# A hybrid decoder step on one core: moving rows at multiples of 64 bytes, norms summed tile by tile between blocks, another order for the WKV phase

## The chip, the cores and the metric

The kernel runs on one core of a Trainium2 chip. The metric is device time in microseconds of one execution; less is better. The kernel before takes 2849.76 us, the median of 3 runs (2849.45 to 2850.34).

## The reference, cut to what matters

One inference step of a decoder trunk with two layers. Layer 0 mixes with RWKV-7, layer 1 with RG-LRU (a gated linear recurrence); each is followed by a causal ConvFFN. Two request groups share the weights: a prompt of 256 tokens and 8 sample rows with carried state, so T = 264 columns. The model is 2048 wide, the FFN 5632.

```
for i in range(2):
    sh_m, sc_m, gt_m, sh_f, sc_f, gt_f = split(silu(c) @ w_mod[i] + b_mod[i])
    h = rms_norm(x, g0) * (1 + sc_m) + sh_m
    out, state = rwkv7_time_mix(h, ...) if i == 0 else rglru_block(h, ...)
    x = x + gt_m * rms_norm(out, g1)
    h = rms_norm(x, g2) * (1 + sc_f) + sh_f
    gt, u = h @ w_gate, h @ w_up
    f = (gelu(causal_dwconv(gt)) * u) @ w_down
    x = x + gt_f * rms_norm(f, g3)
```

The step returns x for both groups and all states (WKV matrices, shift rows, recurrence and convolution states).

## The kernel before, in words

The activations lie with channels on the 128 partitions and the 264 tokens along the row: U0 (the residual) and U1 (a block's output) have 16 tiles of 128 channels. A weight piece is 128 x 1024 numbers, two k-tiles by four output tiles of 128. SyncE loads it raw (L420), ScalarE casts it to a rounded high half wh (L434), and VectorE subtracts to get the low half wl (L435). A ring of four wh and four wl tiles holds split pieces, so a split can run up to four pieces ahead. The moving side is split in the same way (L492, L493) into AH and AL, or ah and al. mm_pieces then issues three products for every pair of k-tile and output tile (L455 wh·xh, L456 wh·xl, L457 wl·xh), 24 matmuls for a piece, into four PSUM banks.

The program is a sequence of stages. Startup loads x (L326), sums its squares over all 16 tiles by matmuls with a matrix of ones (NormPipe, L505 and L506), and computes the first modulation vectors with narrow matmuls against w_mod (wm, L345) and a transpose (L740). Then come the RWKV projections, the WKV phase from about 300 to 713 us, the output projection, and FFN 0 to 1670; the RG-LRU layer to 2021; FFN 1 to 2827; the tail.

The WKV phase is a set of generators, one letter for each kind of job (JOBS), and a text table ORDER says which job takes its next step; with manual_schedule the instructions stand in exactly that order on every engine. Elsewhere the tile framework's scheduler places instructions by their program order and their dependences. Between blocks, w_mod's pieces for later modulation vectors are computed at a fixed pace (wm_pump, paced by mm_group).

Between two blocks lies a junction. out_proj or ffn ends with four groups of pieces; each finished bank is squared (SqAcc.push) and evicted with its gate into U1. The first 12 squares are added up by GpSimd into sqacc, the last four stay apart as tails. rstd_of then sums sqacc and the four tails with five matmuls (L484), takes the square root (L486) and the reciprocal (L488): r1. residual adds U1 * r1 to U0, the sample's columns for all tiles at once (L543, L544), the prompt's two tiles at a time by step on VectorE or GpSimd (L549, L550). residual_and_h then forms the input of the next block without waiting for the next norm: XH and XL hold U0 * sc, split (L580, L581), with the sample's and the shift's columns at the end (xe, L568 to L570), 274 columns; main(p) multiplies piece p with tiles 2p and 2p+1. Beside it the squares of U0 (L577, paired at L582) are summed by norm(p) (L586); after norm(7) the reciprocal r2 (L628) scales the four results, and prep forms AH and AL for all later pieces of the block. There are three such junctions, and the end of the program has the residual part alone.

Of the kernel before, what the change touches and what calls it, by code (L numbers as in the profile page):

```python
# [42 lines left out]
v1 2v0 v1 2s2 2w4 p6 p7 b3 p6 2w5 u4 u5 x1 p6 v1 p6 2v0 2v1 2b2 v0 3q0 d4 b3 v1 q0 2b3 2q0 p7 3b3 q0 2p8 2h0
d4 2p7 p6 2h0 q0 p8 h0 3q0 l8 p8 2p6 b4 4s2 p6 3q0 3b3 p7 s4 p7 2v1 d5 2x2 p7 2l9 3q0 2v2 p7 2v1 p7 q0 h0 v1
2v2 a0 q0 o0 2p6 3p7 w7 2o0 2p6 l11 v3 2p7 2q1 v2 d7 q1 v2 4p9 p8 o0 2h0 2s4 2v2 2q1 v2 2b4 b5 o0 2v2 2p8 v3
a1 3o0 l10 h0 p7 v3 2x2 p9 q0 x2 v3 s4 w6 2s4 4o0 p9 3x2 p8 2x2 w6 p8 2q1 2p8 b4 d6 4q1 b4 2g0 s4 2g0 2p9 3g0
u6 w7 u7 v3 2q1 b4 2g0 3q1 s4 g0 v4 b4 2v4 l10 4v3 d6 d7 2w8 2s6 u8 v4 b4 v3 4q1 2g0 2a0 w9 q0 q1 a0 v3 a0 s6
# [1772 lines left out]
```

## Time and profile before

| what | value |
|---|---|
| median of 3 runs | 2849.76 us (2849.45 to 2850.34) |
| profiled execution | 2848.57 us, span 2846.8 us, mean granted TensorE clock 0.987 |
| TensorE busy | 2740.7 us, 96% of the span |
| VectorE, ScalarE, GpSimd busy | 1753.7, 1358.7, 524.4 us |
| read from memory | 629.42 MB, 226 GB/s over the span |

The span is the time from the first to the last instruction that the profile shows; the execution's time is 1.8 us longer. A busy share is an average over all stages. The chain of waits follows the work that ended last back to what released it, so it tells which engine's time makes up the span.

### The profile page before, as it was taken

The numbers are of one execution on the slowest core, as the hardware profiler recorded it, in microseconds if no ns is written. First come the engines' busy times: TensorE is split into PE (matmuls) and PEld (weight loads), VectorE is DVE, ScalarE is ACT, GpSimd is POOL, SyncE is SP. The second block draws the span as 40 slices with busy tenths as digits, with TensorE's granted clock in tenths as the row PEclk, the third lists the DMA queues.
The fourth block names the chain that finished last, engine by engine and source line by source line (L and its number), as shares of the span: only waits on it lengthen the run. The fifth ranks groups of instructions, "written<-read, shape, count | busy, mean of one in ns | idle before, by whom it ended". The sixth has DMA issues, their size and how long they took to land.

```text
span 2846.8 us, 61582 instructions
## 1 busy us (share of the span) xinstructions
PE 2740.7 (96%) x25820; PEld 2526.2 (89%) x25820; DVE 1753.7 (62%) x2824; ACT 1358.7 (48%) x2187; POOL 524.4 (18%) x1045
## 2 busy tenths in 40 slices
PE   7999999888999999999999999999999999999997
PEld 6899876665989999999999989999899999999997
DVE  5877776876476535545545579775765455455555
ACT  5333435644455434433434459785554444344444
POOL 2111435553121000000000023332210000000002
PEclk9999999999999999999999999999999999999998
DMA  8777558776766666666666665666666555555552
GB/s 330 288 261 244 185 176 246 241 234 215 276 237 232 257 245 238 252 252 255 247 237 252 256 248 199 253 239 237 237 244 252 207 180 178 178 180 184 183 183 76
DMA packets 146566, 648.48 MB, mean 228 GB/s; under 512 B 41152, under 2 KB 60752, under 8 KB 78064
## 3 DMA queue, kind: packets, MB, share of 16 engines
q1 hardware_dynamic: 145216, 641.25, 62.7%
q8 instruction: 202, 3.31, 0.5%
q0 software_dynamic: 1072, 3.30, 0.4%
q14 instruction: 76, 0.62, 0.1%
HBM read 629.42 MB, written 15.07 MB: 226 GB/s over the span
## 4 chain that ended last, share of the span: by engine, by line
PE 86%; DVE 7%; ACT 2%; DMA 2%; issue 1%; POOL 1%; SPq 0%; DVEq 0%; ACTq 0%; POOLq 0%
PE bk L455 18%; PE bk L456 18%; PE bk L457 18%; PE sq L455 7%; PE sq L456 7%; PE sq L457 7%; PE wm L345 5%; DVE wl L435 1%; PE bk L902 1%; ACT wh L434 1%; DVE bt L549 1%; PE bk L908 1%; PE bk L814 0%; PE sq L814 0%; DVE U L550 0%
## 5 line engine op out<-in xcount | busy, mean ns | idle before, releaser
L435 DVE TENSOR_TENSOR wl<-raw,wh 128x1024 fp32r<-128x1024 f32 x444 | 547.6, 1235 | 495.0 <-ACT wh L434 485.8
L434 ACT CAST wh<-raw 128x1024 fp32r<-128x1024 f32 x444 | 464.5, 1048 | 631.6 <-PE bk L456 428.4
L455 PE MATMUL bk<-AH,wh 128*128 128x264 f32 x2352 | 670.6, 285 | 1.4 <-ACT wh L434 1.4
L457 PE MATMUL bk<-AH,wl 128*128 128x264 f32 x2352 | 669.1, 284 | 1.7 <-DVE wl L435 1.6
L456 PE MATMUL bk<-AL,wh 128*128 128x264 f32 x2352 | 668.6, 284 | 0.8 <-DVE AL L493 0.8
L435 DVE TENSOR_TENSOR wl<-rawx,wh 128x1024 fp32r<-128x1024 f32 x310 | 379.3, 1226 | 331.9 <-ACT wh L434 326.8
L434 ACT CAST wh<-rawx 128x1024 fp32r<-128x1024 f32 x310 | 324.4, 1048 | 452.9 <-PE bk L456 332.7
L455 PE MATMUL bk<-ah,wh 128*128 128x264 f32 x1786 | 514.6, 289 | 9.2 <-ACT ah L492 5.5
L457 PE MATMUL bk<-ah,wl 128*128 128x264 f32 x1786 | 510.6, 286 | 0.5 <-DVE wl L435 0.5
L456 PE MATMUL bk<-al,wh 128*128 128x264 f32 x1786 | 510.6, 286 | 0.0
L455 PEld LDWEIGHTS bk<-AH,wh 128*128 128x128 f32 x2352 | 443.3, 188 | 20.7 <-ACT cv L1560 8.4
L457 PEld LDWEIGHTS bk<-AH,wl 128*128 128x128 f32 x2352 | 441.7, 188 | 2.8 <-DVE wl L435 2.8
L456 PEld LDWEIGHTS bk<-AL,wh 128*128 128x128 f32 x2352 | 442.5, 188 | 1.0 <-DVE AL L493 1.0
L455 PEld LDWEIGHTS bk<-ah,wh 128*128 128x128 f32 x1786 | 337.6, 189 | 27.6 <-ACT wh L434 8.1
L457 PEld LDWEIGHTS bk<-ah,wl 128*128 128x128 f32 x1786 | 338.1, 189 | 1.4 <-DVE wl L435 0.8
L456 PEld LDWEIGHTS bk<-al,wh 128*128 128x128 f32 x1786 | 338.4, 189 | 0.6 <-DVE al L493 0.2
L455 PE MATMUL sq<-AH,wh 128*128 128x264 f32 x1040 | 296.7, 285 | 0.1
L456 PE MATMUL sq<-AL,wh 128*128 128x264 f32 x1040 | 295.6, 284 | 0.0
L457 PE MATMUL sq<-AH,wl 128*128 128x264 f32 x1040 | 295.4, 284 | 0.0
L1553 POOL COPY fgs<-gt 128x10 f32<-128x10 f32 x88 | 53.4, 634 | 1307.5 <-ACT gt L1547 1286.2
L455 PEld LDWEIGHTS sq<-AH,wh 128*128 128x128 f32 x1040 | 196.0, 188 | 9.6 <-ACT cv L1560 3.4
L456 PEld LDWEIGHTS sq<-AL,wh 128*128 128x128 f32 x1040 | 195.7, 188 | 0.0
(469 smaller groups left out, 4501.3 us busy)
## 6 DMA issues: line engine op xcount, KB each, us to landing
raw<-in_wst SPq DMA_DIRECT2D x224, 1024.0 KB, 4.9
rawx<-in_wst SPq DMA_DIRECT2D x157, 1024.0 KB, 4.8
raw<-in_wmr SPq DMA_DIRECT2D x72, 1024.0 KB, 7.6
raw<-in_wmr SPq DMA_DIRECT2D x88, 512.0 KB, 5.5
rawx<-in_wmr SPq DMA_DIRECT2D x44, 1024.0 KB, 8.2
raw<-in_wmq SPq DMA_DIRECT2D x23, 1024.0 KB, 4.9
rawx<-in_wmq SPq DMA_DIRECT2D x9, 1024.0 KB, 4.8
lu<-in_lup SPq DMA_DIRECT2D x32, 128.0 KB, 4.8
```

The source lines that it names most:

```text
L345: PE.matmul(ps[32 * g:32 * g + 32, :cols], cs[:, k0 + kk, :], raw[:, (kk * 4 + g) * cols:(kk * 4 + g + 1) * cols], start=(k0 + kk == 0), s ...
L434: S.copy(wh, t)
L435: V.tensor_sub(wl, t, wh.bitcast(F32))
L455: PE.matmul(ps[:, :n], h[:, kk, sl], xh, start=first and kk == 0, stop=False)
L456: PE.matmul(ps[:, :n], h[:, kk, sl], xl, start=False, stop=False)
L457: PE.matmul(ps[:, :n], l[:, kk, sl], xh, start=False, stop=last and kk == 1)
L549: e.tensor_tensor(t, U1[:, j:j + n, :TP], r1[:, None, :TP].to_broadcast([128, n, TP]), op=mult)
L902: PE.matmul(out[HH[(i + turn) % 2]], lhs[HH[i]], rhs[HH[i]], start=start, stop=stop, skip_group_check=True)
L908: PE.matmul(out[q], lhs(r), rhs[r], start=start, stop=stop, skip_group_check=True)
L1553: G.tensor_copy(gs[:, m], gt[:, TP:])
```

## The change

It has five parts.

1. Rows of the moving tiles. AH, AL, ah, al, xh and xl get rows of TA = 272 numbers, of which 264 are used: 1088 bytes instead of 1056. The small tile half grows from 1 to 9 columns, so that what is allocated after it starts at a multiple of 64 bytes. XH and XL (274 columns) stay as they are.
2. ORDER is another permutation of the same jobs for the WKV phase. Which instruction stands where shifts in small steps all through the phase; the set of instructions is the same.
3. Startup: x is loaded in four parts, and all 16 norm steps stand ahead of the modulation pieces.
4. Junctions: in the last group of a block the norm's accumulation begins ahead of the last piece (acc.begin), each bank is squared as soon as its matmuls are issued (hook), the tails are added one by one (add_tail), and the gated evictions of the last two banks wait until after the reciprocal (acc.rest). The two paced pumps stand one piece earlier, and two of the four pumps of the junction move behind its first part. The sample's part is split: VectorE does tiles 0 and 1, GpSimd tiles 2 to 15. The first part of the junction stands in a fixed order on all engines.
5. End: VectorE does all eight residual steps, GpSimd the sample's part, and each step is followed by its output load to memory.

```diff
+TA = 272
...
-s0 g0 p0 l0 2p0 p1 3x0 2l1 l0 p1 g0 5p0 g0 p1 p0 3x0 5p1 p0 w0 p0 l2 2p1 x0 p0 3x0 3p0 2p1 2p0 p2 b0 2p2 2l3
+l0 g0 2p0 s0 x0 g0 2x0 l0 6p0 l1 h0 x0 4p0 2x0 2w0 2p1 b0 l1 3p1 2p0 2p1 l2 3x0 p2 b1 2p1 l2 p1 g0 2p1 p0 2p2
...
-    SP.dma_start(U0[:, :, 1:], I["xT"])
+    for j in range(0, 16, 4):
+        SP.dma_start(U0[:, j:j + 4, 1:], I["xT"][:, j:j + 4])
...
+            if acc and end:
+                acc.begin()
+            mm_pieces(pss, pc, [rhs(2 * q), rhs(2 * q + 1)], q == 0, end, T, hook if end else None)
...
-                elif p == 0:
+                elif p == (2 * pace[0] - 1 if ahead and q >= nk // 2 - 2 else 0):
                     wm_pump(2, False)
-            if ahead and q == nk // 2 - 1:
-                for w in range(ahead):
-                    wm_load(wm_state["i"] + w)
+                    for w in range(ahead):
+                        wm_load(wm_state["i"] + w)
...
+        def begin(s):
+            s.ps = bank()
+            PE.matmul(s.ps[:, :T], onesd, s.acc, start=True, stop=False)
+
+        def add_tail(s, i):
+            PE.matmul(s.ps[:, :T], onesd, s.tail[i], start=False, stop=i == 3)
...
-        step = residual(pool, acc)
-        wm_pump(4)
-        step(V, 0, 2)
-        step(G, 10, 2)
...
-        parts(0)
-        main(0)
-        step(V, 2, 2)
-        step(G, 12, 2)
-        parts(1)
-        norm(0)
-        step(V, 4, 2)
+        with tc.manual_schedule(engines=MANUAL):
+            step, sample = residual(pool, acc)
+            wm_pump(2, False)
+            wm_load(wm_state["i"])
+            wm_load(wm_state["i"] + 1)
+            sample(V, 0, 2)
+            sample(G, 2, 14)
+            step(V, 0, 2)
+            extra(V, 0, 2)
+            halves(0)
+            main(0)
+            step(V, 2, 2)
+            extra(G, 2, 14)
+            halves(1)
+            squares(0)
+            main(1)
+            pairsum(0)
+            step(V, 4, 2)
+            squares(1)
+            pairsum(1)
+            step(G, 10, 2)
+            step(G, 12, 2)
+            norm(0)
+        wm_pump(2, False)
         parts(2)
-        main(1)
...
-            h = a1p([128, T], F32R, "ah", 9)
-            l = a1p([128, T], F32R, "al", 9)
+            h = a1p([128, TA], F32R, "ah", 9)[:, :T]
+            l = a1p([128, TA], F32R, "al", 9)[:, :T]
...
+    for j in range(16):
+        np0.push(U0[:, j, 1:])
     for kp in range(4):
         mod_piece(0, kp)
-        if kp < 2:
-            for j in range(8 * kp, 8 * kp + 8):
-                np0.push(U0[:, j, 1:])
...
+            def hook(m, ps):
+                acc.push(ps[:, :T])
+                if m < 2:
+                    gated(m, ps)
+                else:
+                    acc.rest.append(lambda: gated(m, ps))
+                    acc.add_tail(m - 2)
...
-    AH = ap_([128, 16, T], F32R, "AH")
-    AL = ap_([128, 16, T], F32R, "AL")
+    AH = ap_([128, 16, TA], F32R, "AH")[:, :, :T]
+    AL = ap_([128, 16, TA], F32R, "AL")[:, :, :T]
...
-    for e, j in ((V, 0), (G, 12), (V, 2), (V, 4), (G, 14), (V, 6), (V, 8), (V, 10)):
-        step(e, j, 2)
-    for j in (0, 2, 12, 4, 6, 8, 14, 10):
-        SP.dma_start(O["yT"][:, j:j + 2], U0[:, j:j + 2, 1:])
+    with tc.manual_schedule(engines=MANUAL):
+        step, sample = residual(bp, acc, 8)
+        sample(G, 0, 16)
+        for j in range(0, 16, 2):
+            step(V, j, 2)
+            SP.dma_start(O["yT"][:, j:j + 2], U0[:, j:j + 2, 1:])
```

The line numbers of the kernel after are a little higher: the products are L457 to L459, the casts L436, the low halves L437, the modulation matmuls L347.

How the startup stands on TensorE, from its first matmul, before (L506 is the norm of x, wm the modulation, ah and al the split input):

```order
L506 MATMUL bk<-sq,onesd 128x264 x3
L345 MATMUL wm<-raw,cT 32x128 x16
L506 MATMUL bk<-sq,onesd 128x264 x5
L345 MATMUL wm<-raw,cT 32x128 x16
L506 MATMUL bk<-sq,onesd 128x264 x8
L345 MATMUL wm<-raw,cT 32x128 x16
L345 MATMUL wm<-rawx,cT 32x128 x16
L455 MATMUL bk<-ah,wh 128x264 x4
L455 MATMUL sq<-ah,wh 128x264
```

and after (there the norm is L502):

```order
L502 MATMUL bk<-sq,onesd 128x264 x16
L347 MATMUL wm<-raw,cT 32x128 x48
L347 MATMUL wm<-rawx,cT 32x128 x16
L457 MATMUL bk<-ah,wh 128x264
L458 MATMUL bk<-al,wh 128x264
L457 MATMUL bk<-ah,wh 128x264
L458 MATMUL bk<-al,wh 128x264
L457 MATMUL bk<-ah,wh 128x264
```

All 16 norm matmuls come first, then the 64 modulation matmuls in one run; in the first piece the product with al comes second instead of sixth.

ScalarE at the first junction, from the square root of the norm on, before (XH is the scaled input of the next block, sqb the squares, wh the high half of a weight piece):

```order
L486 ACTIVATE sd<-sq,epsn 128x264
L580 ACTIVATE XH<-U_78,mod_11379 128x256
L569 CAST XH<-xe 128x16x18
L577 ACTIVATE sqb<-U_78 128x528
L580 ACTIVATE XH<-U_78,mod_11379 128x256 x2
L577 ACTIVATE sqb<-U_78 128x528
L580 ACTIVATE XH<-U_78,mod_11379 128x256 x5
L577 ACTIVATE sqb<-U_78 128x528
L580 ACTIVATE XH<-U_78,mod_11379 128x256 x2
L577 ACTIVATE sqb<-U_78 128x528
L580 ACTIVATE XH<-U_78,mod_11379 128x256 x2
L434 CAST wh<-rawx 128x1024 x2
```

and after:

```order
L546 ACTIVATE rs_11701<-sq,epsn 128x264
L1540 ACTIVATE U_10837<-bk,mod_7040 128x256 x2
L590 CAST XH<-xe 128x2x18
L584 ACTIVATE XH<-U_78,mod_11382 128x256 x2
L436 CAST wh<-rawx 128x1024
L590 CAST XH<-xe 128x14x18
L584 ACTIVATE XH<-U_78,mod_11382 128x256 x2
L579 ACTIVATE sqb<-U_78 128x528
L436 CAST wh<-rawx 128x1024
L579 ACTIVATE sqb<-U_78 128x528
L436 CAST wh<-rawx 128x1024 x2
L584 ACTIVATE XH<-U_78,mod_11382 128x256 x3
```

Two evictions follow the square root; four casts of weight pieces stand behind the first four XH rows of the prompt, where before the first stands behind the twelfth.

VectorE at the same place, from the first XL of the prompt's columns on, before (bt and U are the residual steps, XL the low half, sqb the paired squares, wl the low half of a weight piece):

```order
L581 SCALAR_TENSOR_TENSOR XL<-U_78,mod_11379,XH 128x256 x2
L582 TENSOR_TENSOR sqb<-sqb 128x264 x2
L581 SCALAR_TENSOR_TENSOR XL<-U_78,mod_11379,XH 128x256 x2
L549 TENSOR_TENSOR bt<-U_10834,rs_11694 128x512 x2
L550 TENSOR_TENSOR U_78<-U_78,bt 128x2x256 x2
L581 SCALAR_TENSOR_TENSOR XL<-U_78,mod_11379,XH 128x256
L582 TENSOR_TENSOR sqb<-sqb 128x264
L581 SCALAR_TENSOR_TENSOR XL<-U_78,mod_11379,XH 128x256 x2
L582 TENSOR_TENSOR sqb<-sqb 128x264
L549 TENSOR_TENSOR bt<-U_10834,rs_11694 128x512
L581 SCALAR_TENSOR_TENSOR XL<-U_78,mod_11379,XH 128x256 x2
L550 TENSOR_TENSOR U_78<-U_78,bt 128x2x256
```

and after:

```order
L585 SCALAR_TENSOR_TENSOR XL<-U_78,mod_11382,XH 128x256 x2
L437 TENSOR_TENSOR wl<-rawx,wh 128x1024
L560 TENSOR_TENSOR bt<-U_10837,rs_11701 128x512
L561 TENSOR_TENSOR U_78<-U_78,bt 128x2x256
L591 TENSOR_TENSOR XL<-xe,XH 128x14x18
L585 SCALAR_TENSOR_TENSOR XL<-U_78,mod_11382,XH 128x256 x2
L437 TENSOR_TENSOR wl<-rawx,wh 128x1024
L595 TENSOR_TENSOR sqb<-sqb 128x264
L560 TENSOR_TENSOR bt<-U_10837,rs_11701 128x512
L437 TENSOR_TENSOR wl<-rawx,wh 128x1024
L561 TENSOR_TENSOR U_78<-U_78,bt 128x2x256
L595 TENSOR_TENSOR sqb<-sqb 128x264
```

In the stretch after, three low halves of weight pieces stand between the residual steps and the pairs of squares; in the stretch before, none.

## Rows read from the trace of the kernel before

**Rows 1.** The page: the chain that ended last, share of the span by engine.
```profile
PE 86%; DVE 7%; ACT 2%; DMA 2%; issue 1%; POOL 1%; SPq 0%; DVEq 0%; ACTq 0%; POOLq 0%
```

**Rows 2.** The page, groups: casts of weight pieces (xcount, busy us, mean ns).
```profile
L434 ACT CAST wh<-raw 128x1024 fp32r<-128x1024 f32 x444 | 464.5, 1048 | 631.6 <-PE bk L456 428.4
...
L434 ACT CAST wh<-rawx 128x1024 fp32r<-128x1024 f32 x310 | 324.4, 1048 | 452.9 <-PE bk L456 332.7
```

**Rows 3.** In time order, TensorE from 857 (29 rows): start us, us, instruction.
```profile
857.49 0.29 PE L455 MATMUL bk<-AH,wh 128*128 128x264 f32 x1
...
860.89 0.28 PE L456 MATMUL bk<-AL,wh 128*128 128x264 f32 x1
```

**Rows 4.** The same view, 833 to 836, on XH and XL (23 rows).
```profile
833.14 0.30 PE L456 MATMUL sq<-XL,wh 128*128 128x274 f32 x1
...
835.94 0.28 PE L457 MATMUL bk<-XH,wl 128*128 128x274 f32 x1
```

**Rows 5.** The chain in order of time, 0 to 36: start us, us, what.
```profile
1.67 12.45 DMA U<-in_xT
...
14.61 3.01 PE bk L506 x6
...
27.00 0.49 ACT sd L511
...
29.24 0.16 DVE wmtt L740
...
29.41 0.73 DVE U L761 x2
...
33.99 1.25 PE bk L455 x4
```

**Rows 6.** Busy time by stretch, WKV phase: us, busy by engine, PEclk, DMA.
```profile
300.00:720.00 420.00, 379.04 (x6420) 287.31 (x6420) 299.83 (x665) 200.74 (x505) 188.62 (x408) 0.96 0.69 218
```

**Rows 7.** In order of time, TensorE, first junction.
```profile
813.10 1.92 PE L345 MATMUL wm<-raw,cT 128*32 128x512 f32 x16
814.96 0.71 PE L484 MATMUL sq<-sqacc,onesd 128*128 128x264 f32 x2
...
817.38 1.07 PE L345 MATMUL wm<-rawx,cT 128*32 128x512 f32 x8
...
825.37 0.59 PE L455 MATMUL sq<-XH,wh 128*128 128x274 f32 x1 [2.74 <-ACT XH L580]
827.94 0.60 PE L456 MATMUL sq<-XL,wh 128*128 128x274 f32 x1 [1.97 <-DVE XL L581]
```

**Rows 8.** Busy time by stretch, first and third junction.
```profile
820.00:840.00 20.00, 13.89 (x90) 12.31 (x87) 20.00 (x30) 11.61 (x23) 9.40 (x7) 0.83 0.67 279
2026.00:2046.00 20.00, 13.90 (x92) 10.26 (x90) 19.47 (x27) 10.27 (x20) 9.51 (x7) 0.83 0.79 331
```

**Rows 9.** In order of time, VectorE, first junction.
```profile
818.00 1.80 DVE L488 RECIPROCAL rs<-sd 128x264 f32<-128x264 f32 x1 [2.49 <-ACT sd L486]
...
820.05 1.75 DVE L549 TENSOR_TENSOR bt<-U,rs 128x512 f32<-128x512 f32 x1
821.72 1.27 DVE L544 TENSOR_TENSOR U<-U,f 128x128 f32<-128x128 f32 x1
...
836.00 0.68 DVE L549 TENSOR_TENSOR bt<-U,rs 128x512 f32<-128x512 f32 x1
...
844.42 2.35 DVE L435 TENSOR_TENSOR wl<-raw,wh 128x1024 fp32r<-128x1024 f32 x2
```

**Rows 10.** In order of time, the end.
```profile
2826.72 0.61 PE L484 MATMUL bk<-sqacc,onesd 128*128 128x264 f32 x2
...
2829.66 1.80 DVE L488 RECIPROCAL rs<-sd 128x264 f32<-128x264 f32 x1 [1.29 <-ACT sd L486]
...
2839.63 1.28 DVE L549 TENSOR_TENSOR bt<-U,rs 128x512 f32<-128x512 f32 x2
...
2842.75 0.69 DVE L550 TENSOR_TENSOR U<-U,bt 128x512 f32<-128x512 f32 x1
```

More of the change, by code (lines that the diff above doesn't have):

```diff
@@ L43 @@
[L43 to L47, printed above, removed]
@@ L446, in build, with mm_pieces @@
     ws = Stream()
-    def mm_pieces(pss, pc, rhs2, first, last, n=T):
+    def mm_pieces(pss, pc, rhs2, first, last, n=T, hook=None):
         h, l = pc
@@ L457, in mm_pieces, with mm_group @@
                 PE.matmul(ps[:, :n], l[:, kk, sl], xh, start=False, stop=last and kk == 1)
+            if hook:
+                hook(m, ps)
     pace = [0, 0]
-    def mm_group(nk, rhs, bg=None, ahead=0):
+    def mm_group(nk, rhs, bg=None, ahead=0, acc=None, hook=None):
         pss = [bank() for _ in range(4)]
@@ L539, in residual, with sample @@
     def residual(pool, acc, nb=2):
-        r1 = rstd_of(pool, [acc.acc] + acc.tail, "rs1")
+        r1 = pool([128, T], F32, "rs1", 1)
+        S.activation(r1, acc.ps[:, :T], AF.Sqrt, bias=epsn)
+        V.reciprocal(r1, r1)
+        for f in acc.rest:
+            f()
         f8 = pool([128, 16, 8], F32, "f8", 1)
-        V.tensor_tensor(f8, U1[:, :, TP:], r1[:, None, TP:].to_broadcast([128, 16, 8]), op=mult)
-        V.tensor_tensor(U0[:, :, TP + 1:], U0[:, :, TP + 1:], f8, op=add)
+        def sample(e, j, n):
+            x = U0[:, j:j + n, TP + 1:]
+            e.tensor_tensor(f8[:, j:j + n], U1[:, j:j + n, TP:], r1[:, None, TP:].to_broadcast([128, n, 8]), op=mult)
+            e.tensor_tensor(x, x, f8[:, j:j + n], op=add)
         def step(e, j, n):
@@ L550, in step @@
             e.tensor_tensor(x, x, t, op=add)
-        return step
+        return step, sample
     def residual_and_h(acc, sc, sh, AH, AL):
@@ L563, in residual_and_h, with squares, halves @@
         G.tensor_copy(xe[:, :, 8:17], sh)
-        step = residual(pool, acc)
-        wm_pump(4)
-        step(V, 0, 2)
-        step(G, 10, 2)
-        G.tensor_tensor(xe[:, :, :8], U0[:, :, TP + 1:], sc[:, :, 1:], op=mult)
-        S.copy(XH[:, :, TP:], xe)
-        V.tensor_sub(XL[:, :, TP:], xe, XH[:, :, TP:].bitcast(F32))
-        pss = [bank() for _ in range(4)]
-        ms = bank()
         sqs = {}
-        def parts(p):
-            q = pool([128, 2, T], F32, "sqb", 3)
+        def squares(p):
+            q = sqs[p] = pool([128, 2, T], F32, "sqb", 3)
             S.activation(q, U0[:, 2 * p:2 * p + 2, 1:], AF.Square)
+        def halves(p):
             for j in (2 * p, 2 * p + 1):
@@ L581, in parts, with extra, pairsum @@
                 V.scalar_tensor_tensor(XL[:, j, :TP], x, sc[:, j, 0:1], XH[:, j, :TP].bitcast(F32), op0=mult, op1=sub)
-            V.tensor_tensor(q[:, 0], q[:, 0], q[:, 1], op=add)
-            sqs[p] = q
+        def extra(e, j, n):
+            x = slice(j, j + n)
+            e.tensor_tensor(xe[:, x, :8], U0[:, x, TP + 1:], sc[:, x, 1:], op=mult)
+            S.copy(XH[:, x, TP:], xe[:, x])
+            V.tensor_sub(XL[:, x, TP:], xe[:, x], XH[:, x, TP:].bitcast(F32))
+        def pairsum(p):
+            q = sqs[p]
+            V.tensor_tensor(q[:, 0], q[:, 0], q[:, 1], op=add)
+        def parts(p):
+            squares(p)
+            halves(p)
+            pairsum(p)
+        pss = [bank() for _ in range(4)]
+        ms = bank()
         def norm(p):
@@ L686, in build @@
     hka = vres([128, 16], F32, "hka")
-    half = vres([128, 1], F32, "half")
+    half = vres([128, 9], F32, "half")[:, :1]
     def wkv_consts():
```

149 lines of the change are left out of this document (86 added, 63 removed).

## The prediction

> **What bounds the kernel now.** I read the chain of waits first: 86% of the span is TensorE [rows 1]. So almost every matmul costs its spacing, and work elsewhere counts only where TensorE stands still. Two places could pay: the spacing of the long matmul stages, and the holes between them. For the spacing I read the instructions in order of time in stages without holes; for the holes the startup, the three junctions (where one block's residual is formed and the next block starts on it) and the end; for the WKV phase, whose order is a table, busy time by stretch.
>
> The sum is made against the profiled execution: 2848.57 us, of which 2846.8 are span. The median of the runs shown is 2849.76, so 1.2 us are added at the end. 0.2% of that, 5.7 us, is about what a measurement of this kernel can tell from no change.
>
> **Rows at a multiple of 64 bytes.** 754 pieces are split [rows 2] and each feeds 24 matmuls: 18,096. The three junctions take 24 pieces (576 matmuls) from XH and XL, which the change leaves alone; 17,520 remain. A row of 264 fp32 is 1056 bytes, 16.5 times 64, so every second row starts 32 bytes off: 8,760 matmuls. What does an odd start cost? In a stage without holes 28 matmuls on AH and AL take 860.89 − 857.49 = 3.40 us, 121.4 ns each [rows 3]; 264 columns at the full 2.4 GHz are 110.0, so 11.4 are overhead. XH, with 274 columns in 1096-byte rows, seven of eight of which start off 64, takes (835.94 − 833.14)/22 = 127.3 ns, 114.2 of them columns: 13.1 of overhead [rows 4]. So the tile with more odd rows pays more, by an amount that also has other possible sources. Grouping all starts in the late stages by even and odd row gives about 1 ns between them, but there odd rows also precede the change of PSUM bank; in the projections, where the ring of nine tiles separates the two, 0.5 is left, and in the WKV phase the sign turns. I take 0.75: 8,760 × 0.75 = **−6.5 us**; bounds −8.8 (1 ns) and +1 (nothing but noise). Nothing hides this term: these matmuls are the chain.
>
> Of the Trainium skill, SBUF — State Buffer, section Specifications (TRN2), says that the memory is read in lines of 16 bytes and that crossing lines carries the penalty. 1056 is 66 such lines, so by that rule the old rows were already aligned and the term is zero; 1096 is not a multiple of 16, so the rule would also explain XH. The sum by it is 2850.4. The two spacings of [rows 3, 4] cannot separate the two readings; the split of even and odd starts speaks against the rule.
>
> **Startup.** The chain is xT's load (1.67, 12.45 us), squares and norm matmuls from 14.61 with modulation matmuls between them, the square root at 27.00, reciprocal, transpose at 29.24, and the first projection at 33.99 [rows 5]. In four loads xT's first quarter can be squared while the others land. I estimate the norm's start at 10 instead of 14.6 and, with the modulation matmuls moved behind it (the order shows it), the square root at 20 and the reciprocal's end at 22.3 instead of 29.3. But all 16 multiplies by the norm now stand ahead of the transpose: 16 × 0.36 (two in 0.73) = 5.8, to 28.1. From transpose to first matmul it was 4.75 with two multiplies and two more (1.4) inside, so 3.4 to 4 remain: 31.5 to 32. Gain 2 to 2.5, less 0.5 to 1 since the first piece now wants its low half at the second matmul: **−1.6 us**, bounds −3.5 (the multiplies overlap the modulation's arrival) and +0.5 (behind the shared queue xT lands no earlier, and the modulation's loads, issued behind four loads, later).
>
> **The WKV table.** The same jobs in another permutation. TensorE is busy 379.04 of 420 us there [rows 6]. The 41 idle us bound what an order can win, and nothing in the trace ranks two permutations; **0**, bounds −6 and +6 (a seventh of the idle time).
>
> **The junctions**, worked out on the first; E is the end of its last main matmul, 813.1, where the modulation matmuls begin. Before: modulation matmuls, norm from 814.96 to 817.38 (five tiles, 2.42 us), first matmul on XH at 825.37, second at 827.94, dense from there [rows 7]. Busy TensorE is 13.89 of the 20 us after 820, at a granted clock of 0.83; the third junction reads 13.90 at 0.83 [rows 8]: a hole of about 6 us each.
> After: two of the five norm tiles (0.97) and the paced modulation matmuls (1.9) come ahead of E, so E is 2.8 later; from E to the square root it is 1.4 (three tiles, the last square beside the first two) instead of 4.3. The reciprocal starts 0.1 earlier. What is late next is VectorE. The second matmul on XH came 9.9 after the reciprocal's start (827.94 − 818.00) [rows 7, 9]; with 14 of 16 tiles of the sample's part on GpSimd I count about 6.5, so TensorE starts the first piece 3.5 earlier. That is not kept. Before, the halves of the first four pieces were split ahead of the junction; after, of the first two only (the order of ScalarE and VectorE shows it). So four low halves, not two, stand in VectorE's list between the reciprocal and the eighth pair of squares: 2.35 more, by the last row of [rows 9], and two small deferred evictions, 0.3. Off it comes 0.6 of the sample's add, which took 1.27 beside GpSimd. VectorE is busy 20.00 of 20 us there [rows 8], so the pair shifts by about 2.0. Behind that pair TensorE before had all of piece four to do, after only 15 of its 24 matmuls: 9 × 0.127 = 1.1 comes back. ScalarE's cast for piece five waits until piece one has freed its buffer and stands ahead of activations that piece two needs: a wait of 2 to 5 us, but inside the 3.5 by which piece one came earlier. The pumps' loads go onto SyncE's queue one piece earlier and hold up no weight load that is due; the two pumps left over run in the hole, at no cost, or 1.9 if piece zero is ready before them. Sum: −0.1 + 2.35 + 0.3 − 0.6 − 1.1 = **+0.8 each** (0.85), **+2.5 us**; bounds −4 each (two thirds of the hole really goes, because VectorE is contended less) and +5 each (the longer junction, below).
>
> On contention the trace shows the multiply bt at 1.75 us while GpSimd works and at 0.68 alone [rows 9]. Trainium skill, SBUF — State Buffer, section Who interferes with whom: a VectorE instruction with both inputs in SBUF contends with a GpSimd one that reads SBUF, and whichever comes second is blocked. The trace agrees. By that rule 14 tiles on GpSimd are no free move: two more steps of VectorE would be held, 2 × 1.07, and with 2.1 more per junction the sum would be 2850.2.
>
> **The end.** From the norm to the reciprocal it is 2.9 [rows 10]; 0.97 of it moves ahead of E and 1.9 remain, so nothing is won there. The eight residual steps all run on VectorE, 16 instructions at 0.64 (two in 1.28) = 10.2, and GpSimd's one sample part holds one or two of them, 1.07 each, 1.5; before, it is 12.0 from the reciprocal's end, 2831.46, to 2843.44 [rows 10]: **−0.3 us**, bounds −1.5 and +1.
>
> Sum: −6.5 − 1.6 + 0 + 2.5 − 0.3 = −5.9, so 2842.7 for the profiled execution and, with 1.2, **2843.9** for the median.
>
> **Rivals.**
> *Rows are no cost* (0.20): the odd starts' 1 ns belongs to the change of bank. For it, the 0.5 in the projections and the sign in WKV; against it, XH's larger overhead. Then −5.9 + 6.5 = +0.6: 2850.4, no change.
> *The holes close* (0.15): the earlier start survives in all three. For it, 6 us of hole each; against it, VectorE's 20.00 of 20. −4 instead of +0.8, three times: 2829.5.
> *The junction becomes longer* (0.17, the other side): VectorE's list carries 2.65 more, two more of its steps are held at 1.75 instead of 0.68 (2.1), nothing comes off, and piece two's wait lies behind the others: +4.8 each, three times 4.0 over the forecast, 2855.9. For it, VectorE's full list; against it, the 9 matmuls. It decides from 4.7 each with the rows' gain, from 2.5 without it.
> *The new table is worse or better* (0.10): ±6, 2838 or 2850. Not told apart beforehand.
> *Forecast* (0.38): 2843.9, own range 2838 to 2850.
> That the rows don't lie at 64 after the change is excluded: 1088 = 17 × 64, and the small tile ahead of the later ones is padded so that they start there too.
>
> **Numbers.** Faster by over 5.7 (below 2844.1): half of the forecast (0.20), the holes (0.15), half of the table (0.05), and of the rows and the long junction what a smaller hole gives back (0.07): 0.47. Slower (above 2855.5): half of the long junction as priced and what of it comes with half or no rows' gain (0.12), a part of the rows and table cases (0.08): 0.20. Same 0.33. The range 2830 to 2857 leaves out the best end of the closing holes and the worst of the long junction.
>
> **What would show it.** Rows: the spacing on AH in a stage without holes falls from 121.4 to about 121.0 and every long stage shortens by 0.3%, the last FFN by 2.5 us; if it stays, that term fails. Startup: first projection at 31.5 to 32.5. Junctions: second matmul on XH 3.5 us sooner, then idle time before pieces two and four "<- ACT XH" and "<- DVE sqb"; if TensorE has no such waits, the holes case is right. End: the stretch from the last norm's first matmul behind E to the end shorter, about 19 us. The forecast is wrong if all stages keep their length and the total stays within 1 us, or if a junction stretch grows by over 3 us.

## The result, and the profile after

| | median us | runs | ratio to before |
|---|---|---|---|
| before | 2849.61 | 4 (2848.56 to 2850.34) | |
| after | 2878.63 | 4 (2872.09 to 2885.13) | 1.0104, 95% [1.008, 1.0128] |

The kernel became 29 us slower; forecast was 2843.9 with a range of 2830 to 2857. The profiled execution of after is the one of 2874.46 us (span 2872.7).

To see where the time went I use the casts of weight pieces on ScalarE as milestones: there are 754 in both kernels and they are the same pieces in the same order. The table gives the length of each stretch less its length in before. Before reaches the ends of these stretches at 70.5, 273.4, 724.5, 798.5, 929.6, 1656.2, 1826.2, 1981.6, 2151.0 and 2788.7 (the starts of casts 12, 72, 96, 120, 156, 384, 432, 480, 528 and 744), and its last instruction at 2846.8. The other rows are the experiments below.

| | start | proj. | WKV | out | junct. 1 | FFN 0 | junct. 2 | LRU | junct. 3 | FFN 1 | end | sum |
|---|---|---|---|---|---|---|---|---|---|---|---|---|
| after | −1.6 | −0.8 | +1.0 | +0.1 | +6.7 | +2.0 | +9.1 | +0.9 | +7.0 | +2.6 | −0.9 | +25.9 |
| rows only | −1.9 | −0.8 | −3.2 | +0.1 | +0.3 | +2.0 | +0.5 | +0.9 | +0.9 | +2.6 | −0.2 | +1.1 |
| rows of ah, al, xh, xl | −0.4 | −0.7 | −2.7 | +0.1 | −0.2 | −1.5 | +0.2 | 0.0 | +0.7 | −1.2 | −0.2 | −6.2 |
| junctions and end | −1.7 | 0.0 | −0.2 | 0.0 | +6.4 | 0.0 | +8.1 | +0.1 | +7.0 | 0.0 | −0.5 | +19.2 |
| junction, free order | +0.6 | 0.0 | +0.2 | 0.0 | +2.3 | 0.0 | +4.2 | 0.0 | +2.6 | 0.0 | −0.5 | +9.5 |
| sum by tile only | −1.2 | 0.0 | −0.2 | 0.0 | +1.1 | 0.0 | +2.3 | 0.0 | +2.3 | 0.0 | −0.5 | +3.8 |
| after, splits ahead | −1.4 | −0.8 | +11.1 | +0.1 | +5.0 | +2.0 | +5.5 | +0.8 | +3.7 | +2.6 | −0.9 | +27.7 |
| table only | −1.1 | 0.0 | +10.6 | 0.0 | +0.6 | 0.0 | +0.2 | 0.0 | +0.8 | 0.0 | 0.0 | +11.1 |
| startup and end | −2.6 | +0.1 | +3.0 | 0.0 | 0.0 | 0.0 | +0.7 | 0.0 | +1.1 | 0.0 | −1.0 | +1.2 |
| what gained, together | −1.0 | −0.8 | +4.9 | +0.1 | +0.1 | −1.5 | +0.1 | 0.0 | +0.6 | −1.2 | −1.2 | 0.0 |

Long stretches whose code is the same repeat to 0.1 us between kernels (FFN 0 and FFN 1 read 0.0 in five rows), so a single profile measures them. The start (−1.9 to +0.6 without any change to it) and the WKV phase (−3.2 to +4.9 with the old table) do not repeat. The junctions repeat to about 1 us: where their code is unchanged, ten profiles (the six in section 4 among them) read −0.2 to +1.4 for one and −0.1 to +2.4 for the three together, +1.3 on average.

Of after's 25.9 us in this profile, 22.7 are in the three junctions, 5.5 in the FFN and LRU stages, 1.0 in the WKV phase; start, projections and end give 3.3 back.

**Startup.** TensorE in order of time in after (start us, us, instruction, idle time before it), the answer to [rows 5]:

```profile
7.85 10.27 PE L502 MATMUL bk<-sq,onesd 128*128 128x264 f32 x32 [7.85 <-ACT sq L501]
...
24.66 1.93 PE L347 MATMUL wm<-rawx,cT 128*32 128x128 f32 x32 [3.09 <-DMA rawx<-in_wmq]
31.37 0.59 PE L457 MATMUL bk<-ah,wh 128*128 128x264 f32 x1 [4.78 <-ACT wh L436]
```

and VectorE:

```profile
26.66 0.32 DVE L775 STREAM_TRANSPOSE wmtt<-wm 128x128 f32<-128x128 f32 x1 [0.16 <-PE wm L347]
```

The norm starts at 7.85 (I had said 10), the first projection at 31.37 (31.5 to 32). The modulation's last matmuls wait 3.09 us for their load, though it was issued sooner than in before (at 7.87, not 8.80); why it lands so late is not shown. It costs little: VectorE multiplies by the norm until 26.50, and the transpose behind both waits 0.16 for the modulation. From the transpose to the first projection it is 4.7, where I had left 3.4 to 4.

**Junction 1.** Busy time by stretch of 10 us, before and then after: us, busy by engine in the order TensorE, weight loads, VectorE, ScalarE, GpSimd, then the granted clock, DMA share and GB/s.

```profile
820.00:830.00 10.00, 3.89 (x22) 2.51 (x19) 10.00 (x14) 4.76 (x11) 6.56 (x5) 0.73 1.01 428
830.00:840.00 10.00, 10.00 (x70) 9.80 (x70) 10.00 (x17) 6.85 (x13) 2.84 (x2) 0.92 0.32 131
840.00:850.00 10.00, 10.00 (x73) 9.67 (x72) 9.97 (x16) 6.09 (x11) 1.36 (x2) 1.00 0.50 173
```

```profile
820.00:830.00 10.00, 7.30 (x39) 6.66 (x40) 8.71 (x12) 6.14 (x11) 4.93 (x5) 0.83 0.87 362
830.00:840.00 10.00, 5.37 (x25) 3.99 (x24) 10.00 (x13) 5.71 (x12) 4.66 (x3) 0.82 0.29 105
840.00:850.00 10.00, 10.00 (x62) 9.57 (x61) 7.77 (x18) 5.79 (x10) 0.00 (x0) 0.84 0.28 105
```

After enters this junction 1.4 us sooner (the first four columns of the table, unrounded), so equal times are not quite equal places. From 820 to 830 after is ahead, 7.30 us against 3.89. From 830 to 840 it stands half the time, where before is busy throughout; and the granted clock stays at 0.82 to 0.84 to the end, where before is back at full speed (of two levels, 1.2 and 2.4 GHz, a share of each stretch runs at the lower). In the last stretch both are busy throughout, with 62 matmuls against 73. TensorE in order of time in after, the answer to [rows 7]:

```profile
821.58 0.39 PE L457 MATMUL sq<-XH,wh 128*128 128x274 f32 x1 [1.92 <-ACT XH L584]
822.10 0.40 PE L458 MATMUL sq<-XL,wh 128*128 128x274 f32 x1
...
832.26 0.68 PE L606 MATMUL bk<-sqb,onesd 128*128 128x264 f32 x2 [0.88 <-DVE sqb L595]
834.94 0.68 PE L606 MATMUL bk<-sqb,onesd 128*128 128x264 f32 x2 [2.00 <-DVE sqb L595]
...
837.86 1.25 PE L606 MATMUL bk<-sqb,onesd 128*128 128x264 f32 x2 [1.76 <-DVE sqb L595]
...
847.97 0.48 PE L457 MATMUL sq<-XH,wh 128*128 128x274 f32 x1
...
849.76 0.61 PE L606 MATMUL bk<-sqb,onesd 128*128 128x264 f32 x2
```

The first two matmuls of the junction come at 821.58 and 822.10, 3.8 and 5.8 sooner than in before; less the 1.4 of head start that is 2.4 and 4.4. Then the first three norms (L606) wait for their pairs of squares, 0.88, 2.00 and 1.76; all but two matmuls of piece two stand behind them in TensorE's order. Piece four starts at 847.97 and the last norm at 849.76; in before the last norm stands ahead of piece four, which starts at 845.08. VectorE in the same stretch, the answer to [rows 9], after and, last, the eighth pair of squares in before:

```profile
826.03 2.51 DVE L585 SCALAR_TENSOR_TENSOR XL<-U,mod,XH 128x256 fp32r<-128x256 f32 x2 [0.24 <-ACT XH L584]
828.46 2.31 DVE L437 TENSOR_TENSOR wl<-rawx,wh 128x1024 fp32r<-128x1024 f32 x1
830.70 1.42 DVE L595 TENSOR_TENSOR sqb<-sqb 128x264 f32<-128x264 f32 x1
...
832.64 1.21 DVE L437 TENSOR_TENSOR wl<-rawx,wh 128x1024 fp32r<-128x1024 f32 x1
...
834.72 1.75 DVE L560 TENSOR_TENSOR bt<-U,rs 128x512 f32<-128x512 f32 x1
836.40 1.40 DVE L595 TENSOR_TENSOR sqb<-sqb 128x264 f32<-128x264 f32 x1
...
842.25 1.22 DVE L437 TENSOR_TENSOR wl<-rawx,wh 128x1024 fp32r<-128x1024 f32 x1
845.70 0.89 DVE L585 SCALAR_TENSOR_TENSOR XL<-U,mod,XH 128x256 fp32r<-128x256 f32 x2 [2.23 <-ACT XH L584]
...
849.12 0.42 DVE L595 TENSOR_TENSOR sqb<-sqb 128x264 f32<-128x264 f32 x1
```

```profile
844.08 0.42 DVE L582 TENSOR_TENSOR sqb<-sqb 128x264 f32<-128x264 f32 x1
```

The first pair of squares takes 1.42 (0.42 alone), two XL before it 2.51 (0.87) and a low half 2.31 (1.23), all while GpSimd does two residual steps one after the other, from 825.6 to 831.8; beside GpSimd's next step, from 834.6, bt takes 1.75 (0.68) and the third pair 1.40. Low halves stand between the squares. At 845.70 VectorE itself waits 2.23 for XH. The eighth pair comes at 849.12, 32.5 us after the reciprocal's start (816.64); in before it is 26.1 (844.08 − 818.00 [rows 9]). What VectorE waits for stands behind a cast on ScalarE:

```profile
831.35 1.04 ACT L436 CAST wh<-rawx 128x1024 fp32r<-128x1024 f32 x1 [2.01 <-PE bk L458]
...
843.67 1.05 ACT L436 CAST wh<-rawx 128x1024 fp32r<-128x1024 f32 x1 [2.93 <-PE bk L458]
...
845.17 0.89 ACT L584 ACTIVATE XH<-U,mod 128x256 fp32r<-128x256 f32 x2
```

The casts at 831.35 and 843.67, of pieces five and six, wait 2.01 and 2.93 for TensorE to be done with pieces one and two and free their buffers, with XH rows behind them: TensorE waits for VectorE, VectorE for ScalarE, ScalarE for TensorE.

**Long stages.** Busy time in two stretches inside FFN 0 and FFN 1; the number in brackets behind TensorE's time counts its matmuls. Before, then after:

```profile
900.00:1600.00 700.00, 700.00 (x5724) 655.67 (x5724) 350.38 (x453) 279.96 (x350) 39.55 (x113) 1.00 0.67 248
2200.00:2760.00 560.00, 560.00 (x4598) 558.42 (x4597) 297.57 (x376) 238.47 (x297) 31.21 (x89) 1.00 0.52 184
```

```profile
900.00:1600.00 700.00, 700.00 (x5704) 657.27 (x5704) 348.45 (x450) 279.95 (x350) 39.50 (x113) 1.00 0.66 247
2200.00:2760.00 560.00, 560.00 (x4579) 556.84 (x4578) 295.24 (x375) 236.96 (x296) 31.32 (x90) 1.00 0.52 186
```

TensorE is busy throughout and does fewer matmuls in the same time, 5704 against 5724 and 4579 against 4598: 0.4% slower spacing, where I had forecast 0.3% faster. Split by tile, the mean start-to-start time on AH and AL after 870 us rose from 121.6 to 122.6 ns (10,000 pairs of starts), in the projections on ah and al it fell from 122.0 to 121.4 (960 pairs from 200 to 400 us).

### The profile page after: what moved, and what is told of

It reads as the page before. It is cut to its first block, busy times and chain, and to the rows that moved or that the text cites. A ratio compares the mean times of both kernels' runs of the same rounds, so it can differ in the third digit from the quotient of the medians.

```text
span 2872.7 us, 61599 instructions
## 1 busy us (share of the span) xinstructions
PE 2761.6 (96%) x25820; PEld 2540.3 (88%) x25820; DVE 1754.2 (61%) x2832; ACT 1355.8 (47%) x2188; POOL 519.9 (18%) x1049
## 4 chain that ended last, share of the span: by engine, by line
PE 73%; DVE 4%; ACT 3%; issue 1%; DMA 1%; POOL 0%; SPq 0%; DVEq 0%; ACTq 0%; POOLq 0%
PE bk L457 16%; PE bk L459 16%; PE bk L458 15%; PE sq L457 6%; PE sq L459 6%; PE sq L458 6%; PE wm L347 4%; DVE wl L437 1%; ACT bt L616 1%; ACT wh L436 1%; PE bk L936 1%; PE bk L942 0%; ACT AH L488 0%; PE bk L1272 0%; PE bk L606 0%
## 5 line engine op out<-in xcount | busy, mean ns | idle before, releaser
L437 DVE TENSOR_TENSOR wl<-raw,wh 128x1024 fp32r<-128x1024 f32 x444 | 546.9, 1233 | 498.2 <-ACT wh L436 490.8
L436 ACT CAST wh<-raw 128x1024 fp32r<-128x1024 f32 x444 | 464.5, 1047 | 626.7 <-PE bk L458 417.8
L459 PE MATMUL bk<-AH,wl 128*128 128x264 f32 x2352 | 673.4, 286 | 5.2 <-DVE wl L437 5.1
L457 PE MATMUL bk<-AH,wh 128*128 128x264 f32 x2352 | 674.8, 287 | 0.0
L437 DVE TENSOR_TENSOR wl<-rawx,wh 128x1024 fp32r<-128x1024 f32 x310 | 382.3, 1235 | 335.8 <-ACT wh L436 331.5
L436 ACT CAST wh<-rawx 128x1024 fp32r<-128x1024 f32 x310 | 324.3, 1047 | 451.8 <-PE bk L458 333.8
L457 PE MATMUL bk<-ah,wh 128*128 128x264 f32 x1786 | 514.3, 288 | 9.3 <-ACT wh L436 9.3
L459 PE MATMUL bk<-ah,wl 128*128 128x264 f32 x1786 | 509.0, 285 | 1.4 <-DVE wl L437 1.4
L457 PEld LDWEIGHTS bk<-AH,wh 128*128 128x128 f32 x2352 | 444.3, 189 | 18.5 <-ACT cv L1613 9.2
L459 PEld LDWEIGHTS bk<-AH,wl 128*128 128x128 f32 x2352 | 442.8, 188 | 7.3 <-DVE wl L437 7.3
L457 PEld LDWEIGHTS bk<-ah,wh 128*128 128x128 f32 x1786 | 337.8, 189 | 27.7 <-ACT wh L436 14.2
L459 PEld LDWEIGHTS bk<-ah,wl 128*128 128x128 f32 x1786 | 337.1, 189 | 2.2 <-DVE wl L437 2.0
L457 PE MATMUL sq<-AH,wh 128*128 128x264 f32 x1040 | 298.7, 287 | 0.2 <-DVE shw L681 0.2
L459 PE MATMUL sq<-AH,wl 128*128 128x264 f32 x1040 | 297.1, 286 | 0.0
L457 PEld LDWEIGHTS sq<-AH,wh 128*128 128x128 f32 x1040 | 196.4, 189 | 10.4 <-ACT wh L436 3.4
```

Of the source, the lines that this page charges most:

```text
L436: S.copy(wh, t)
L437: V.tensor_sub(wl, t, wh.bitcast(F32))
L457: PE.matmul(ps[:, :n], h[:, kk, sl], xh, start=first and kk == 0, stop=False)
L459: PE.matmul(ps[:, :n], l[:, kk, sl], xh, start=False, stop=last and kk == 1)
```

## The experiments

Beside the experiments before ran from 2843 to 2858 us; each ratio is against the runs beside it and taken over all of them, so that it can differ from the ratio of the two medians. Kernels run once are judged by the table alone.

**1. The parts alone: rows, junctions, table.** The rows (with the square root written in place, to make room):

```diff
+TA = 272
-    AH = ap_([128, 16, T], F32R, "AH")
+    AH = ap_([128, 16, TA], F32R, "AH")[:, :, :T]
...
-            h = a1p([128, T], F32R, "ah", 9)
+            h = a1p([128, TA], F32R, "ah", 9)[:, :T]
```

> The kernel before with part 1 alone: rows of 272 for AH, AL, ah, al, xh, xl (the square root is written in place into the reciprocal's tile, for space). Theory A (from the trace after: spacing on ah falls from 122.0 to 121.4 ns, on AH rises from 121.5 to 122.6): +4 to +6 us in all, the stages up to 860 us shorter by 0.3%, the FFN stages longer by 0.3 to 0.4%. Rival (the prediction's term): -6 us. Second rival (the slower FFN stages of the kernel after come from elsewhere): within 1 us of before.

Measured: 2857.82 (10 runs) against 2852.31, 1.002 [1.0008, 1.0031], +2.3 to +8.8 us. FFN 0 +2.0, FFN 1 +2.6, LRU +0.9, projections −0.8, as in after to 0.1; together +4.7. Theory A holds, +4 to +6; the whole of the rows costs time.

Junctions and end alone, that is after with these three parts undone:

```diff
-TA = 272
+TA = T
-    for j in range(0, 16, 4):
-        SP.dma_start(U0[:, j:j + 4, 1:], I["xT"][:, j:j + 4])
+    SP.dma_start(U0[:, :, 1:], I["xT"])
...
-l0 g0 2p0 s0 x0 g0 2x0 l0 6p0 l1 h0 x0 4p0 2x0 2w0 2p1 b0 l1 3p1 2p0 2p1 l2 3x0 p2 b1 2p1 l2 p1 g0 2p1 p0 2p2
+s0 g0 p0 l0 2p0 p1 3x0 2l1 l0 p1 g0 5p0 g0 p1 p0 3x0 5p1 p0 w0 p0 l2 2p1 x0 p0 3x0 3p0 2p1 2p0 p2 b0 2p2 2l3
```

> The kernel before with parts 4 and 5 alone (norm summed tile by tile, fixed order in the junctions, end on VectorE); rows, table and startup as before. Theory J (the junctions carry most of the loss): +18 to +24 us, each junction 6 to 8 us longer than before, the end 1 us shorter. Rival (the junction shift is only the spacing and the clock of the whole kernel): under +6 us.

Measured: 2868.88 (4 runs) against 2852.31, 1.0063 [1.0048, 1.0078], +16.6 us by the medians and +13.7 to +22.2 by the interval; by the table +21.5 in the junctions (20 if the mean of unchanged junctions, +1.3, is taken off) and nothing in the long stages; the end −0.5. Theory J, with one junction a little over its 8 and the end half of what it said.

The table alone (its text exchanged in before, nothing else):

```diff
-s0 g0 p0 l0 2p0 p1 3x0 2l1 l0 p1 g0 5p0 g0 p1 p0 3x0 5p1 p0 w0 p0 l2 2p1 x0 p0 3x0 3p0 2p1 2p0 p2 b0 2p2 2l3
+l0 g0 2p0 s0 x0 g0 2x0 l0 6p0 l1 h0 x0 4p0 2x0 2w0 2p1 b0 l1 3p1 2p0 2p1 l2 3x0 p2 b1 2p1 l2 p1 g0 2p1 p0 2p2
```

> The kernel before with the new table for the WKV phase alone. Theory: 0 to +2 us, since in the trace after the phase from 322 to 724 us is about 1 us longer. Rival (the table is what makes the kernel after scatter from 2872 to 2885 us): +1 to +12 us with a scatter over the rounds of several us.

Measured: 2858.76 (10 runs, 2850.15 to 2865.20) against 2852.31, 1.0026 [1.0011, 1.0041]. That is +3.1 to +11.7 us: my 0 to +2, read from one execution, fails, and the rival's size holds. In the profile the phase is 10.6 longer, and 1.0 and 11.1 in the two other profiles with this table; with the old table 13 profiles lie from −3.2 to +4.9. Busy time from 325 to 725 in before and here:

```profile
325.00:725.00 400.00, 359.08 (x6285) 268.77 (x6284) 282.53 (x634) 189.13 (x485) 182.29 (x395) 0.96 0.70 221
```

```profile
325.00:725.00 400.00, 353.63 (x6196) 263.55 (x6195) 275.95 (x623) 178.46 (x469) 176.13 (x393) 0.94 0.68 212
```

In 400 us TensorE is idle 5.5 us more, and the granted clock is 0.94 instead of 0.96. Over the whole stretch of the table (6615 matmuls in both) its idle time is 50.7 against 45.2 and its busy time 411.0 against 405.9: of the 10.6, about half is idle time and half is the same work taking longer. Scatter is not the new table's alone: before scatters by 15 us as well beside it.

**2. What in the junction costs it.** First, after with the split of weight pieces run one piece further ahead at the end of a block:

```diff
             if acc and end:
+                ws.split_to(ws.i + 2)
                 acc.begin()
```

> The kernel after with one line more: at the last piece of a block's last group the split of weight pieces runs one piece further ahead, so that three pieces instead of two are split when the junction begins. Theory J1 (TensorE waits in the junction because casts and low halves of later pieces stand in the fixed order of ScalarE and VectorE): 2 to 3 us less per junction, 6 to 9 us less than after. Rival J2 (the order of residual steps, squares and norms alone makes the waits): within 2 us of after.

Measured: 2876.18 (4 runs, 2866.81 to 2876.63) against after's 2878.63, not told apart; in this profile the WKV phase alone is 11.1 longer than in before and hides the gain. By the stages the three junctions are 1.6, 3.6 and 3.3 shorter, 8.4 together, as J1 said. But not by J1's mechanism alone: in junction 1 TensorE waits at the norms as long as in after (the list of who waited for whom: us in total, times, longest), in after and then here:

```profile
PE bk L606 <- DVE sqb L595: 4.6, 3, 2.0
PE sq L457 <- ACT XH L584: 1.9, 1, 1.9
```

```profile
PE bk L607 <- DVE sqb L596: 4.7, 3, 2.0
PE sq L457 <- ACT XH L585: 1.5, 1, 1.5
```

Of the 1.6 us in this junction 0.7 are shorter waits for XH and XL; the rest is no wait that the list shows. So the split pieces and the waits at the norms are two costs, not one. In the other two junctions VectorE's own idle time up to the eighth pair of squares falls from 3.4 and 2.7 us to 0.9 and 0.9, in this one only from 3.6 to 3.2.

Second, the junction on before with its first part placed by the scheduler (division of the sample part and written order as in after):

```diff
-        with tc.manual_schedule(engines=MANUAL):
+        if True:
             step, sample = residual(pool, acc)
```

> Parts 4 and 5 on the kernel before, but the first part of the junction placed by the scheduler instead of in a fixed order; the split of the sample part stays. Theory J1: the scheduler pulls splits and halves ahead, junctions within 3 us of before each. Rival J2 (the division of the sample part and the order in which the steps are written make the waits): +5 each or more, as with the fixed order.

Measured: junctions +2.3, +4.2, +2.6 (9.1 together, against 21.5 in the fixed order). J1's bound of 3 is missed in one of three, J2 falls. The eighth pair of squares comes 27.2, 27.2 and 26.5 us behind the reciprocal in the three junctions, against 32.5, 32.3 and 31.6 in after and 26.1 in before. The waits in junction 1 are fewer:

```profile
PE bk L605 <- DVE sqb L594: 2.4, 1, 2.4
PE sq L456 <- ACT XH L589: 2.3, 1, 2.3
```

Third, the tile-by-tile sum alone, with the old body of the junction behind it:

```diff
-        with tc.manual_schedule(engines=MANUAL):
...
-            sample(V, 0, 2)
-            sample(G, 2, 14)
-            step(V, 0, 2)
-            extra(V, 0, 2)
-            halves(0)
-            main(0)
...
+        sample(V, 0, 16)
+        step(V, 0, 2)
+        step(G, 10, 2)
+        extra(G, 0, 16)
+        parts(0)
+        main(0)
...
```

> The kernel before with the norm between blocks summed tile by tile in the last piece (and the end on VectorE), but the junction itself in the old order, placed by the scheduler, with the whole sample part on VectorE. Theory J1 (the fixed order of the junction and the splits that it holds back cost the time, not the sum): junctions within 2 us of before each, against +6.4 to +8.1. Rival J3 (the early sum itself, with its matmuls and pumps ahead of the last matmul, costs it): +5 each or more.

Measured: +1.1, +2.3, +2.3. J1's 2 us is missed by 0.3 in two of three, J3 falls. No wait at a norm in the first junction, but the early start is gone as well:

```profile
PE sq L456 <- ACT XH L583: 4.4, 1, 4.4
PE sq L457 <- DVE XL L584: 1.3, 1, 1.3
```

In before these two waits were 2.7 and 2.0 [rows 7]. So of 21.5 us, 5.6 come with the sum (and the moved pumps and evictions that go with it), 3.5 with the division of the sample part and the written order, 12.4 with fixing that order on all engines, of which one more piece split ahead gives 8.4 back. These are single profiles and steps taken in one order: 12.4 is far outside the scatter of the junctions, 5.6 and 3.5 are not far outside it.

**3. Startup and end.** Part 3 as in the diff of the change, and the end on before:

```diff
-    step = residual(bp, acc, 8)
-    for e, j in ((V, 0), (G, 12), (V, 2), (V, 4), (G, 14), (V, 6), (V, 8), (V, 10)):
-        step(e, j, 2)
...
+        step = residual(bp, acc, 8, G)
+        for j in range(0, 16, 2):
+            step(V, j, 2)
+            SP.dma_start(O["yT"][:, j:j + 2], U0[:, j:j + 2, 1:])
```

> The kernel before with the startup's part 3 and the end's eight steps on VectorE alone. The prediction's terms: first projection 1.6 us sooner, end 0.3 us shorter. Rival (the kernels without the new startup reach the first stages 0.7 to 1.9 us sooner as well, so the gain is how the loads happen to land): stages after the startup not over 0.5 us ahead of those kernels.

Measured: start −2.6, end −1.0. Four profiles with the new startup read −2.6, −1.6, −1.4 and −1.0, mean −1.7; twelve without it, before among them, −1.9 to +0.7, mean −0.5. So about 1 us is the startup's; the rival holds for the rest of the 1.7.

**4. Why the rows matter.** Rows of 272 for ah, al, xh, xl alone:

```diff
-            h = pool([128, T], F32R, "ah", 14)
+            h = pool([128, TA], F32R, "ah", 14)[:, :T]
```

> The kernel before with rows of 272 for ah, al, xh, xl alone; AH and AL stay at 264. Theory A (ah gains, AH loses by longer rows): no stage longer; projections 0.7 us shorter, each FFN 1 to 2 us shorter, since only the second matrix of an FFN reads ah. Rival A2 (the FFN stages lose by ah as well, or by where the tiles come to lie): FFN stages longer again by 2 us each.

Measured (one run, 2842.39 beside 2848.44): projections −0.7, FFN 0 −1.5, FFN 1 −1.2, no long stage longer. Theory A. By subtraction the long rows of AH and AL cost +3.6 in FFN 0 and +3.8 in FFN 1.

Is it where AL lies behind AH? In before AH starts at 64 modulo 256 and AL 16896 bytes on, with the long rows 17408. A gap makes the same distance with old rows, and 64 bytes another one with long rows:

```diff
     AH = ap_([128, 16, T], F32R, "AH")
+    ap_([128, 128], F32, "gap")
     AL = ap_([128, 16, T], F32R, "AL")
```

> The kernel before, AH and AL with their old rows of 264, but 512 bytes left free between them, so that AL lies 17408 bytes behind AH, as it does with rows of 272 (before: 16896). Theory D (the distance between AH and AL, not the rows' start, sets the spacing): the FFN stages 2 to 4 us longer each, as with the long rows. Rival S (the step from row to row does): within 0.5 us of before.

> The kernel before with rows of 272 for AH and AL alone, and 64 bytes left free between them: AL lies 17472 bytes behind AH, all rows at multiples of 64. Theory D: the loss of 3.6 to 3.8 us per FFN stage changes sign or shrinks by more than half. Rival S: FFN stages 3.5 to 4 us longer than before, as rows_only less rows_small gave.

Measured: with the old rows FFN 0 and FFN 1 read 0.0 and 0.0 (Rival S); with the long rows +0.1 and +0.5 (Theory D). So D fails in the first and S in the second, and three more places were tried: with the long rows the gap behind both tiles, by which both start 64 bytes lower (AH and AL both at 0 modulo 256), and the old rows with gaps of 64 and 128 bytes (AH at 0 and at 192, AL at 64):

```diff
     AL = ap_([128, 16, TA], F32R, "AL")[:, :, :T]
+    ap_([128, 16], F32, "gap")
```

> Rows of 272 for AH and AL, and 64 free bytes below both: each starts 64 bytes lower than in the version without the gap, AL stays 17408 behind AH. Theory D2 (AL's rows against AH's modulo 256 bytes set the spacing): the loss stays, +3.6 us in FFN 0 and +3.8 in FFN 1. Rival B (the start of AH's rows modulo 256 does): under +0.5 each, as with the gap between them.

> The old rows of 264 with 64 bytes left free between AH and AL: AL lies 16960 behind AH. Theory D2: the spacing on AH changes, FFN stages at least 1 us shorter or longer each. Rival R (only rows that repeat after four are touched): FFN stages within 0.5 us of before.

> The same with 128 free bytes, AL 17024 behind AH. Theory D2: the spacing changes again by another amount, at least 1 us per FFN stage. Rival R: within 0.5 us of before.

| rows | AH, AL modulo 256 | FFN 0 | FFN 1 |
|---|---|---|---|
| 264 | 64, 64 (before; also the gap of 512) | 0.0 | 0.0 |
| 264 | 0, 64 | −0.1 | −0.2 |
| 264 | 192, 64 | +1.3 | +1.5 |
| 272 | 64, 64 (as in after; by subtraction) | +3.6 | +3.8 |
| 272 | 0, 64 | +0.1 | +0.5 |
| 272 | 0, 0 | +0.1 | −0.3 |

Rival B, the start of AH's rows, holds for the long rows; D2 falls there. For the old rows neither D2 nor R does wholly: 64 bytes change nothing, 128 change 1.3 and 1.5. A gap moves the tiles ah and al of the FFN by as many bytes too, so the traces were split by tile: on AH and AL the mean start-to-start time is 122.7 ns with the long rows at 64, 64 and 121.6 to 121.8 at 0, 64 and 0, 0, while on ah and al, with their old rows, it stays within 0.2 of before in the three kernels with a gap of 64 bytes. The change is on AH and AL. What is shown is that the place of the rows within 256 bytes moves a stage by 3.3 to 4.1 us, and that a multiple of 64 is not what decides. Why is open.

**5. What gained, together.** Before, with rows of 272 for the small tiles, the new startup and the new end (diffs above).

> The kernel before with what gained: rows of 272 for ah, al, xh, xl, the new startup, and the end's eight steps on VectorE; AH, AL, the table and the junctions as before. From the stages of the runs so far: -4 (ah rows) -1 (startup) -0.5 to -1 (end), so 5 to 6 us below before, 0.998. Rival: the scatter of the WKV phase (several us between executions) hides it, interval including 1.

Measured: 2844.87 (12 runs) against 2848.55 (17 runs), 0.9981 [0.997, 0.9992]: 3.7 us faster than before by the medians, 2.3 to 8.5 by the interval, in which the 5 to 6 expected lie; the rival, an interval that includes 1, falls. By the table it is −3.9 outside start and WKV phase, and the latter is 4.9 longer in this profile.

## Why the prediction was wrong

- **Junctions: the step that failed.** I gave +0.8 each; run alone they cost +6.4 to +8.1. The first half of the working held: less the head start, the reciprocal of junction 1 starts within 0.1 of before, as forecast, and the second matmul on XH comes 5.5 behind it instead of 9.9 (6.5 forecast). The step that failed is the next one, VectorE's list up to the eighth pair of squares, which I made 2.0 longer, with 1.1 of that coming back. In after the pair comes 6.4, 6.2 and 5.5 us later behind the reciprocal in the three junctions (of the table's 6.7, 9.1 and 7.0 that leaves 0.3, 2.8 and 1.5 elsewhere). Of the 6.4 in junction 1, 3.5 are idle time of VectorE, which I had put at nothing because it was busy 20.00 of 20 in before: 2.23 in one wait for XH, the rest in four short ones. The other 2.9 stand against the 2.0 forecast. I also let the first three norms pass without a wait; they hold TensorE for 4.6 us, with most of piece two queued behind them. And "inside the 3.5 by which piece one came earlier" was wrong for the casts: piece five's waits 2.01, as forecast, but piece six's then waits 2.93 for piece two, and VectorE stands behind that; one piece split further ahead gives 8.4 back over three junctions. Nor had I a term for the granted clock, 0.82 to 0.84 over the 30 us in which before goes from 0.73 back to 1.00.
- **Contention: moved more than added.** VectorE's instructions that take over 0.2 us longer beside GpSimd than alone lose 6.0 us in junction 1 of after, and 4.4 in before, where two more (1.27 and 1.49 us) have no undisturbed one of their form beside them. So the two more held steps that I priced at 2.1 do not show in the sum. What changed is the place: 3.7 of it now lie right ahead of the first pair of squares and in it, after TensorE has begun. The rival of the longer junction named the place, a full list with piece two's wait behind it, with 4.8 each, below the lowest measured, and I held it at 0.17.
- **Rows: the sign of a term.** −6.5 forecast, about +5 measured in the stages that repeat. On ah and al the gain came (−0.7, −1.5 and −1.2 us). On AH and AL I took the same, and the long rows cost 3.6 and 3.8 in the FFNs. The difference of about 1 ns between even and odd rows that I had read from before does not follow from the multiple of 64 on these tiles: rows of the same alignment, 64 bytes on, differ by 3.3 to 4.1 us per stage. The rule of 16-byte lines (Trainium skill, SBUF — State Buffer, Specifications (TRN2)) would have all these versions alike, since all rows start at multiples of 32 bytes; the measurement decides against it as well.
- **Table: 0 taken, about +6.5 measured** ([1.0011, 1.0041]), at the edge of the ±6 that I allowed. I had no means to rank the two, and a share of the idle time was no bound on a loss: half of the 10.6 in the profile is busy time.
- **Startup: right in place, about 1 of the 1.6 in size.** First projection at 31.37. That the table reads −1.6 for after, just as forecast, is luck: kernels without the change start 0.5 sooner than before on average. **End:** −0.5 (junctions and end) to −1.2 (what gained, together) against −0.3.
- **The range**, 2830 to 2857, took each bound as independent with gains as likely as losses; junctions, rows and table all went up together.

Added up from the parts run alone: 21.5 + about 5 + 6.5 − 1 − 0.5 = about 31, against 29 measured [23, 36]; with the scatter of the single profiles the agreement is no closer than a few us.

## What to carry to other kernels

A start that comes sooner is worth only what the next engine can follow with: count every instruction that a fixed order puts between the first matmul and the next one on each engine, and look for a circle (here a matmul that waits for a sum, a sum behind a split, a split behind a cast, the cast behind the matmul). If a fixed order ends a stretch, the work that the scheduler used to pull ahead across its edge must be written ahead by hand. Before a tile's rows are padded for alignment, try the tile alone, and at two places in memory.
